# A streaming encoder layer on one core: the low halves of branch B's weights move from VectorE to GpSimd, and the spare pieces are dealt out as two lists

## The chip, the core and the metric

The kernel runs on one core of one Trainium2 chip. Five engines work side by side and meet at semaphores: TensorE (PE, its weight loads PEld), VectorE (DVE), ScalarE (ACT), GpSimd (POOL) and SyncE (SP), which here issues nearly all DMAs in one queue. Each engine takes its instructions in the order in which the program lists them. The metric is the time of one execution on the device in microseconds (us); lower is better. A difference is told as a ratio or in us against the kernel before.

## What is computed

One layer over 2048 new frames ("prompt", 16 tiles of 128 rows) and 8 running streams of 16 frames each ("sample", one tile of 128 rows) with 512 cached positions. A normalised and modulated input is projected; two attention branches run on it; both are gated, projected, merged and added to the input. Branch A is differential softmax attention (4 heads of 2 x 64), branch B stick-breaking attention (8 heads of 64):

```python
def stick_breaking_attention(q, k, v, qpos, kpos):
    z = jnp.einsum('bqhd,bkhd->bhqk', q, k,
                   preferred_element_type=jnp.float32) * (HEAD_DIM_B ** -0.5)
    mask = kpos[None, :] < qpos[:, None]
    log_1m = jnp.where(mask, jax.nn.log_sigmoid(-z), 0.0)
    log_a = jax.nn.log_sigmoid(z) + lax.cumsum(log_1m, axis=3, reverse=True) - log_1m
    a = jnp.where(mask, jnp.exp(log_a), 0.0)
    o = jnp.einsum('bhqk,bkhd->bqhd', a, v, preferred_element_type=jnp.float32)
    return o.astype(v.dtype)
```

The kernel forms the weight as a product of two numbers: sigmoid(z), and the running product of sigmoid(-z) over the later keys. Matrix products want more than 16 bits of precision here, so an f32 operand is written as two f16 numbers, a high half (the value rounded) and a low half (what the rounding lost).

## The kernel before

The work has three stages: normalisation and modulation of the input (to about 140 us), attention (to about 1850 us), and the merge with the samples' attention (to the end).

Attention runs in 8 units, `u` = 0 to 7. An even unit is one head of branch A (`kind` 0), an odd unit is two heads of branch B (`kind` 1). A unit has 17 steps: the samples' projection (`t == NT`, with `NT` = 16), then the 16 tiles `t` = 0 to 15. Step `t` computes scores of 128 queries against the first `t + 1` blocks of 128 keys, so a unit's steps grow. The value products of a step are issued two steps later (`PV_LAG` = 2). The projections (`line`, function `take`) run some five steps ahead of the scores (`LEAD`), so the last steps of a B unit carry projections of the next unit, an A unit, whose rotation (L479, L481, L484) is on POOL and whose splits (L304, L473) are on ACT and DVE.

What a B step does for each of its two heads, from the last chunk of 512 keys to the first: scores on PE into a PSUM bank (L649, L650); two sigmoids on ACT (L123), one into the SBUF buffer `p`, one in place in PSUM; a scan on DVE (L626, function `stick`) that reads the bank, writes the running product to the SBUF buffer `n` and frees the bank. Chunks are gathered in segments of up to 8 blocks, 1024 keys. When a segment has been scanned, `stick_weights` multiplies `p` by `n` on POOL (L632), and `turn` makes the f16 halves in the room of `n`: the high half by a cast on ACT (L582), the low half by a subtraction on DVE (L583). SP then issues one DMA (L590) that transposes both halves into `wt`, from which PE takes its weights for the value products (L710, L711). There are 24 segments for each head of a unit, so 192 in all, 80 of them of 1024 keys and 16 of each shorter length. There are six buffers each for `p` and `n` (`SC_BUFS`), five for `wt` (`WT_BUFS`), three PSUM banks for scores. The samples' tile uses the same functions later, with 8 segments of 640.

The order on each queue is not the program's text alone: the framework lays the instructions out by its own estimate of times, and deals semaphores accordingly. The main loop (from about L1288) decides which pieces a step is given.

Beside this, each step is given pieces of other work. `prepare_unit` (`back`) loads, scales and splits the next unit's weights in the first nine steps of a unit (half of the first parts of these splits are on POOL, L301, the second on DVE, L304). `norms` (`spare`) holds 82 entries in one list: 48 norms (one load of 512 KB and one sum of squares on ACT, L281) of branch weights, output weights and cached values; then 34 stages for cached keys. A stage loads one piece of 512 KB, squares another on ACT, and splits a third: a sum over partitions on PE, four tiny instructions on DVE that make a scale (L867 to L870), the high half on POOL (L301), the low half on DVE (L304), and a store of 512 KB (L875). `spare_at` names the 81 steps that get an entry each, the first of them two: in unit 0 from `t` = 7, in units 2, 4 and 6 all 16 tiles, in units 1, 3 and 5 `t` < 8. In this order the norms take units 0 to 3 and six steps of unit 4; the key stages take the last ten steps of unit 4, eight of unit 5 and all of unit 6.

## Time and profile before

| | |
|---|---|
| median of 3 runs | 2340.57 us (2337.23 to 2343.8) |
| the profiled execution's own time | 2343.11 us |
| its span, first to last instruction | 2341.3 us |
| mean granted TensorE clock | 0.967 of full speed |
| DMA packets moved | 445.30 MB, 190 GB/s on average |

A busy share is the part of a stretch in which an engine executes. A busy PE is not PE at its peak, because matmuls overlap in the records. In a row of groups the columns are the line, the engine, the operation, the buffers written and read, the shape, the count, the busy time, the mean of one in ns, the idle time of the engine just before them and what ended it. In a row of waits they are who waited, for whom, us in total, times, and the longest. In a row of a stretch they are its ends, its length, and the busy time and count of each engine named in its header. A row of a line's instructions gives the shortest, median and longest duration in ns, when the first and the last began, and the shapes.

### The profile page before, as it was taken

To read this page: it belongs to the slowest core of one execution; us is meant where nothing else is said; L and a number is where in the kernel's file an instruction comes from. 1 tells how busy PE (TensorE), PEld (TensorE's weight loads), DVE (VectorE), ACT (ScalarE), POOL (GpSimd) and SP (SyncE) were. 2 spreads that over 40 slices of the span, in tenths; PEclk is the share of its full clock that TensorE was granted. 3 is DMA by queue.
4 is the path that set the end of the run, shared out by engine and by line. 5 is a ranking of instruction groups with operands and counts; after the bars stand their busy time and mean duration, and the time that the engine had idled before them with its cause. 6 is when DMAs were issued, how large, how long until landed. Compare 5 with 4: busy or idle time off the path is not lost. (4 is left out here: it accounts for less than half of the span.)

```text
span 2341.3 us, 41804 instructions
## 1 busy us (share of the span) xinstructions
PE 2102.5 (90%) x14752; PEld 1128.2 (48%) x14752; DVE 1745.7 (75%) x3795; ACT 1624.2 (69%) x3228; POOL 702.6 (30%) x610
## 2 busy tenths in 40 slices
PE   5998899988999898898989988889998689899998
PEld 3654454545555454444544544445454344444443
DVE  4658766779776777977777798887778878677663
ACT  4868677777877777786676786766578666556541
POOL 1223012356400244641033366311335312122111
PEclk8999999999999999999999999999999799999999
DMA  9768667799886778977777789966577899788421
GB/s 335 267 212 222 137 144 174 158 211 198 217 200 146 176 158 202 199 183 183 206 192 185 168 192 229 250 167 165 147 162 168 182 271 260 210 223 215 145 96 55
DMA packets 805827, 445.30 MB, mean 190 GB/s; under 512 B 537354, under 2 KB 744506, under 8 KB 805104
## 3 DMA queue, kind: packets, MB, share of 16 engines
q1 hardware_dynamic: 804668, 442.24, 75.5%
q8 instruction: 115, 1.88, 0.3%
q14 instruction: 96, 0.79, 0.1%
q10 hardware_dynamic: 948, 0.39, 0.1%
HBM read 228.82 MB, written 86.02 MB: 134 GB/s over the span
## 5 line engine op out<-in xcount | busy, mean ns | idle before, releaser
L632 POOL TENSOR_TENSOR sc_p<-sc_p,sc_n 128x127 f32<-128x127 f32 (+7 forms) x192 | 311.3, 1625 | 673.8 <-DVE sc_n L626 650.8
L438 PE MATMUL ps_mm<-wb,hs 128*128 128x512 f16 x1530 | 399.3, 383 | 6.6 <-DMA hs<-hT_d 3.8
L438 PE MATMUL ps_mm<-wa,hs 128*128 128x512 f16 x1590 | 404.3, 380 | 0.8 <-DVE v L304 0.5
L438 PEld LDWEIGHTS <-hs 128*128 128x128 f16 x3120 | 275.6, 99 | 257.0 <-issue 7.8
L626 DVE TENSOR_TENSOR_SCAN sc_n<-ps_s,sc_n,zero_t 128x512 f32<-128x512 f32 x192 | 245.4, 1278 | 72.9 <-ACT ps_s L123 69.2
L649 PE MATMUL ps_s<-k,qst 128*128 128x512 f16 (+3 forms) x640 | 226.7, 355 | 47.2 <-DVE sc_n L626 28.8
L583 DVE TENSOR_TENSOR sc_n<-sc_p,sc_n 128x128 f16<-128x128 f32 (+7 forms) x192 | 213.0, 1115 | 48.2 <-ACT sc_n L582 47.9
L514 PEld LDWEIGHTS <-hs 128*128 128x128 f16 x1632 | 157.1, 99 | 186.9 <-issue 9.6
L514 PE MATMUL ps_t<-wb,hs 128*128 128x512 f16 x1020 | 244.5, 382 | 1.5 <-DVE qst L542 1.5
L123 ACT ACTIVATE sc_p<-ps_s,usc 128x512 f32<-128x512 f32 (+3 forms) x320 | 204.2, 638 | 47.8 <-PE ps_s L650 36.3
L650 PE MATMUL ps_s<-k,qst 128*128 128x512 f16 (+3 forms) x640 | 226.3, 355 | 0.0
L710 PE MATMUL ps_o<-v,wt 128*128 128x128 f16 x1088 | 174.3, 226 | 56.7 <-DMA wt<-sc_n 56.7
L582 ACT CAST sc_n<-sc_p 128x128 f16<-128x128 f32 (+7 forms) x192 | 155.4, 814 | 69.4 <-POOL sc_p L632 69.2
L123 ACT ACTIVATE ps_s<-ps_s,usc 128x512 f32<-128x512 f32 (+3 forms) x328 | 199.2, 607 | 0.0
L1391 PE MATMUL ps_o<-wo,wa 128*128 128x512 f16 x816 | 185.1, 382 | 6.0 <-ACT wo L299 5.3
L710 PEld LDWEIGHTS <-wt 128*128 128x128 f16 x1088 | 106.4, 102 | 122.5 <-DMA wt<-sc_n 68.9
L514 PE MATMUL ps_t<-wa,hs 128*128 128x512 f16 x612 | 157.3, 389 | 6.0 <-ACT qst L542 6.0
L711 PE MATMUL ps_o<-v,wt 128*128 128x64 f16 x1088 | 160.9, 199 | 0.0
L1362 PE MATMUL ps_mm<-wa,wb 128*128 128x512 f16 x510 | 144.2, 390 | 7.8 <-DVE wa L1364 3.4
L568 DVE TENSOR_SCALAR_CACHE_REDUCE sc_p<-ps_s,usc 128x512 f32<-128x512 f32 (+3 forms) x160 | 106.2, 664 | 35.3 <-PE ps_s L650 19.5
L626 DVE TENSOR_TENSOR_SCAN sc_n<-ps_s,zero_t 128x128 f32<-128x128 f32 (+3 forms) x128 | 104.1, 815 | 37.3 <-ACT ps_s L123 36.6
L711 PEld LDWEIGHTS <-wt 128*128 128x128 f16 x1088 | 104.3, 101 | 54.9 <-issue 0.8
(374 smaller groups left out, 4460.3 us busy)
## 6 DMA issues: line engine op xcount, KB each, us to landing
hs<-hT_d SPq DMA_DIRECT2D x130, 512.0 KB, 4.4
g_d<-gt SPq DMA_DIRECT2D x68, 256.0 KB, 4.8
out_dram<-pr SPq DMA_DIRECT2D x204, 64.0 KB, 2.2
wa<-in_w_in_dram SPq DMA_DIRECT2D x40, 256.0 KB, 6.0
o_d<-o SPq DMA_DIRECT2D x136, 64.0 KB, 2.5
wb<-g_d SPq DMA_DIRECT2D x17, 512.0 KB, 3.8
wa<-g_d SPq DMA_DIRECT2D x17, 512.0 KB, 3.4
hs<-o_d SPq DMA_DIRECT2D x17, 512.0 KB, 3.8
```

The lines of the kernel that those rows point to most:

```text
L123: i = S.activation(**kw)
L438: T.matmul(box["p"], box["h"][:, hi, k, :], U["w"][k][:, wi, :], start=(n == 0), stop=(n == 3 * KT - 1))
L514: T.matmul(box["g"][:, 0:gw], box["h"][:, hi, k, :], U["wg"][k // per][:, k % per, wi, :], start=(j == 0), stop=(j == 3 * KT - 1))
L582: S.copy(out=hi, in_=src)
L583: V.tensor_tensor(out=lo, in0=src, in1=hi, op=ALU.subtract)
L626: V.tensor_tensor_scan(out=dst[:, lo : lo + n][:, ::-1], data0=src[:, 0:n][:, ::-1], data1=zero_t[:, 0:1].to_broadcast([P, n]), initial=fi ...
L632: G.tensor_tensor(out=p[:, 0:m], in0=p[:, 0:m], in1=n[:, 1 : m + 1], op=ALU.mult)
L649: T.matmul(p[:, 0:n], qst[:, c, :], kk[:, c, 0:n], start=True, stop=False)
L650: T.matmul(p[:, 0:n], qst[:, 2 + c, :], kk[:, c, 0:n], start=False, stop=not diag)
L710: T.matmul(po[:, c * P : (c + 1) * P], wt[:, wj, :], vt[:, c, :, :], start=first, stop=False)
L711: T.matmul(po[:, c * P : c * P + 64], wt[:, nb + wj, :], vt[:, c, 0, :], start=False, stop=last)
L1391: T.matmul(po, st["y"][:, yi * 8 + k, :], wo[j * 4 + k // 2][:, wi, k % 2, :], start=(n == 0), stop=(n == 3 * KT - 1))
```

## The change

The low half of a B segment is computed on GpSimd in place of VectorE for the 16 prompt tiles; for the samples it stays on VectorE. High half, product, scan, transpose and buffers stay as they are; the scans go on reading PSUM. And `norms` returns two lists in place of one: `spare`, the 48 norms, and `cached`, the 34 key stages. Each has its own set of steps. The norms go to unit 0 from `t` = 7 (nine of them), to `t` = 9 to 15 of units 1 to 5 (seven each), and what is left, four, to the first tiles of unit 6. The key stages go to `t` < 8 of units 1, 3 and 5 (eight each) and to `t` = 9 to 12 of units 2, 4 and 6 (four, four, and the last two). The amount of work is the same.

```diff
@@ turn @@
         if scale is None:
             S.copy(out=hi, in_=src)
-            V.tensor_tensor(out=lo, in0=src, in1=hi, op=ALU.subtract)
+            (G if job["t"] < NT else V).tensor_tensor(out=lo, in0=src, in1=hi, op=ALU.subtract)
         else:
             split(hi, lo, src, scale, S)
@@ norms @@
-        return [lambda x=x: one(*x) for x in srcs] + [lambda k=k: stages(k) for k in range(len(todo) + 2)]
+        return [lambda x=x: one(*x) for x in srcs], [lambda k=k: stages(k) for k in range(len(todo) + 2)]
...
-    spare = norms()
+    spare, cached = norms()
...
-    def spare_at(u, t):
-        return u < 7 and t < NT and (t >= 7 if u == 0 else u % 2 == 0 or t < 8)
+    def norm_at(u, t):
+        return u < 7 and t < NT and (t >= 7 if u == 0 else t >= 9 or u == 6)
+
+    def keys_at(u, t):
+        return u in (1, 3, 5) and t < 8 or u in (2, 4, 6) and 9 <= t < 13
@@ main loop @@
-            if u == 7 and not back and not spare and len(branch_weights) > 1:
+            if u == 7 and not back and not spare and not cached and len(branch_weights) > 1:
                 branch_weight()
...
-            if spare and spare_at(u, t):
-                left = sum(spare_at(*step) for step in steps[n:])
-                for _ in spare[: -(-len(spare) // left)]:
-                    spare.pop(0)()
+            for todo, here in ((spare, norm_at), (cached, keys_at)):
+                if todo and here(u, t):
+                    left = sum(here(*step) for step in steps[n:])
+                    for _ in todo[: -(-len(todo) // left)]:
+                        todo.pop(0)()
...
-        if at[0] == len(line) and not pieces and not spare:
+        if at[0] == len(line) and not pieces and not spare and not cached:
```

## The prediction, as it was put on record before the run

> **What bounds the kernel now.** I read the totals first, then the busy time by stretch, then what TensorE (PE) waited for in the stretches that stood out, and last the two instructions that the edit touches.

> ```profile
> span 2341.3 us, 41804 instructions
> PE 2102.5 (90%) x14752; PEld 1128.2 (48%) x14752; DVE 1745.7 (75%) x3795; ACT 1624.2 (69%) x3228; POOL 702.6 (30%) x610
> ```

> PE is busy nine tenths of the span, so at most 239 us could be won. GpSimd (POOL) has most room. An average hides where the room is, so here are the units 2 to 6 of attention, cut at the first evacuation of each (even units are branch A, odd ones B), the third unit being one B unit from 739 to 971 us:

> ```profile
> core 0: us, PE busy (x) PEld busy (x) DVE busy (x) ACT busy (x) POOL busy (x), PEclk, DMA share, GB/s
> 554.00:739.00 185.00, 178.42 (x1257) 98.24 (x1256) 141.67 (x385) 142.98 (x321) 41.88 (x44) 0.99 0.80 196
> 739.00:971.00 232.00, 211.56 (x1513) 113.14 (x1512) 178.27 (x272) 183.10 (x378) 98.42 (x80) 0.99 0.80 177
> 971.00:1173.00 202.00, 186.72 (x1278) 103.67 (x1276) 157.11 (x429) 142.39 (x314) 51.53 (x54) 0.96 0.79 195
> 1173.00:1416.00 243.00, 219.80 (x1538) 116.63 (x1537) 194.83 (x315) 184.22 (x382) 112.77 (x88) 0.98 0.80 184
> 1416.00:1624.00 208.00, 186.38 (x1286) 103.40 (x1284) 166.71 (x459) 139.71 (x311) 59.87 (x60) 0.98 0.81 209
> ```

> And inside the B units, the middle of unit 1, then the last steps of units 1, 3, 5 and 7:

> ```profile
> 380.00:480.00 100.00, 98.86 (x662) 51.54 (x661) 73.38 (x117) 74.64 (x149) 35.13 (x28) 1.00 0.70 150
> 480.00:580.00 100.00, 84.94 (x669) 46.94 (x668) 89.22 (x140) 77.87 (x157) 60.55 (x48) 0.98 0.97 211
> 900.00:1000.00 100.00, 83.72 (x662) 45.71 (x660) 90.56 (x142) 79.09 (x163) 60.76 (x48) 1.00 0.95 210
> 1340.00:1440.00 100.00, 85.48 (x692) 48.05 (x691) 90.31 (x142) 78.46 (x156) 64.53 (x50) 0.99 0.88 203
> 1780.00:1850.00 70.00, 44.58 (x391) 27.29 (x389) 63.96 (x84) 56.19 (x96) 38.40 (x22) 0.76 0.80 170
> ```

> In the middle PE is the bound (98.9 of 100). In the ends it is not: VectorE (DVE) is at 89 to 91 of 100, at 64.0 of 70 in the last, and PE loses 15.1, 16.3, 14.5 and 25.4 us, 71 us together. What PE waited for there, first from 480 to 580 us, then from 1780 to 1850 us:

> ```profile
> PE ps_s L649 <- DVE sc_n L626: 8.5, 9, 2.6
> PE ps_t L527 <- DVE k L304: 3.0, 3, 1.2
> PE ps_o L710 <- DMA wt<-sc_n: 2.9, 2, 2.0
> ...
> PE ps_o L710 <- DMA wt<-sc_n: 15.1, 11, 3.3
> PE ps_s L649 <- DVE sc_n L626: 5.8, 8, 1.3
> ```

> Scores wait for a PSUM bank that a scan on DVE frees, and the value products for the transpose of weights whose low half DVE made. So in the ends DVE is the bound, and only there.

> **The low halves.** 192 subtractions (L583) leave DVE and go to POOL. What they take on DVE in the first and last of these ends, and beneath that the products (L632) on POOL in the same two:

> ```profile
> 480.00:580.00 100.00, 26.86 (x15) 0.98 0.97 211
> 1780.00:1850.00 70.00, 19.37 (x15) 0.76 0.80 170
> ...
> 480.00:580.00 100.00, 31.02 (x15) 0.98 0.97 211
> 1780.00:1850.00 70.00, 33.23 (x15) 0.76 0.80 170
> ```

> DVE falls from 89.2 to 62.4 in the first and from 64.0 to 44.6 in the last. For the price on POOL I take its product, which like the subtraction has two inputs:

> ```profile
> L632 POOL TENSOR_TENSOR sc_p<-sc_p,sc_n x192: 404/1768/3094, 322.9 to 1841.1; 128x1024 f32<-128x1024 f32 x64, 128x127 f32<-128x127 f32 x16, 128x255 f32<-128x255 f32 x16, 128x383 f32<-128x383 f32 x16
> L632 POOL TENSOR_TENSOR dsc<-dsc x8: 1315/1328/1677, 1943.1 to 2204.4; 128x639 f32<-128x639 f32 x8
> L632 POOL TENSOR_TENSOR sc_p<-sc_p,sc_n 128x1024 f32<-128x1024 f32 x64 | 141.4, 2210 | 216.8 <-DVE sc_n L626 212.2 <-DVE sc_e L232 2.7 <-DVE csc L870 1.9
> L301 POOL TENSOR_SCALAR wa<-wb,csc 128x1024 f16<-128x1024 f32 x11 | 12.9, 1169 | 63.4 <-issue 37.8 <-DVE csc L870 25.6
> L583 DVE TENSOR_TENSOR sc_n<-sc_p,sc_n x192: 260/1084/2994, 326.3 to 1846.8; 128x1024 f16<-128x1024 f32 x80, 128x128 f16<-128x128 f32 x16, 128x256 f16<-128x256 f32 x16, 128x384 f16<-128x384 f32 x16
> L583 DVE TENSOR_TENSOR dsc<-dsc x8: 807/812/820, 1949.7 to 2210.3; 128x640 f16<-128x640 f32 x8
> ```

> Undisturbed, POOL takes 404 ns for 127 columns and 1315 for 639, so 1.78 ns a column, and 2.00 us for 1024. Eighty of that and sixteen each of the seven shorter lengths (0.41, 0.63, 0.86, 1.09, 1.32, 1.54, 1.77, sum 7.6) make 160 + 122 = 282 us. No subtraction from f32 and f16 of this length is in the trace. Bounds: the one-input POOL row above, 1.17 us for 1024, gives 60% of that, 165 us; the disturbed mean of 2.21 gives 312 us. I take 282, since two inputs are what the products have. POOL goes from 703 to about 985 us.

> The product rows spread from 404 to 3094 ns and DVE's from 260 to 2994, and that is a second price:

> ```profile
> L583 DVE TENSOR_TENSOR sc_n<-sc_p,sc_n 128x1024 f16<-128x1024 f32 x9 | 19.2, 2135 | 0.7 <-ACT sc_n L582 0.7
> L626 DVE TENSOR_TENSOR_SCAN sc_n<-ps_s,sc_n,zero_t 128x512 f32<-128x512 f32 x17 | 21.7, 1274 | 0.4
> L473 DVE SCALAR_TENSOR_TENSOR qbuf<-rot,sq,qbuf 128x128 f16<-128x128 f32 x7 | 6.3, 893 | 0.0
> L626 DVE TENSOR_TENSOR_SCAN sc_n<-ps_s,sc_n,zero_t 128x512 f32<-128x512 f32 x192 | 245.4, 1278 | 72.9 <-ACT ps_s L123 69.2
> L473 DVE SCALAR_TENSOR_TENSOR qbuf<-rot,sq,qbuf 128x128 f16<-128x128 f32 x68 | 37.5, 551 | 9.2 <-ACT qbuf L472 9.0
> ```

> The first three are from 500 to 580 us, the others from the whole run. DVE's own rate is (812 - 260) / 512 = 1.08 ns a column, 1.23 us for 1024, but in the end of a unit the subtraction takes 2.14, and the query's split 893 ns against 551. The scan, whose data is in PSUM, takes 1274 against 1278. So DVE and POOL hold each other up where both read two operands from SBUF, and the scans are out of it. After the change the pair product and low half no longer collide; the splits of queries, keys and weights that stay on DVE meet a busier POOL.

> [...]

> Now the end of a unit, 480 to 580 us, engine by engine. DVE 62.4. POOL 60.6, plus 15 low halves, as many as products, mostly of 768 to 1024 columns (1.54 to 2.00), so about 1.85 (27.8), minus what its 15 products lost to collisions (31.0 - 27.8 = 3.2): 85. PE 84.9, ACT 77.9. The floor is 85, a gain of 15. But three engines near 80% that wait for one another in order do not overlap fully, so I take 40% of it, 6 us; ends: 15 gained, or 4 lost if POOL pays the disturbed 2.21 us throughout and its queue adds a wait per step. Three such ends: -18 (-45 to +12). The last, 70 us long: POOL 38.4 + 27.8 - 5.4 = 61 against DVE's 44.6, so POOL is the new bound and 9 us are free; I take -5 (-9 to +4).

> Each low half also lengthens the chain scan, product, cast, low half, transpose, value product. In the short first steps of a B unit nothing covers that; from 321 to 421 us the only wait of PE was

> ```profile
> PE ps_o L710 <- DMA wt<-sc_n: 7.1, 3, 4.4
> ```

> The four shortest lengths cost POOL 0.41, 0.63, 0.86, 1.09 against DVE's 0.26, 0.40, 0.54, 0.67: 1.1 us more, for two heads 2.2 a unit, 9 in four units. A low half that waits for ACT's cast also holds back everything behind it on POOL: the next product, the rotations of branch A's projections, the halving of a key piece. On SP's queue the transpose waits for POOL now, with the next loads behind it. And the halving of a key piece, now among the products of units 1 and 3 too, holds POOL up itself:

> ```profile
> POOL wa L301 <- DVE csc L870: 83.6, 14, 16.8
> L582 ACT CAST sc_n<-sc_p 128x128 f16<-128x128 f32 (+7 forms) x192 | 155.4, 814 | 69.4 <-POOL sc_p L632 69.2
> ```

> Six us on average over 14 times, though unit 5 has this already and loses no more PE time to it than unit 3 (23 and 20 us). I take +7 (0 to +25). In the middle of the units PE at 98.9 covers it.

> **The two lists.** Nothing is added: 48 norms and 34 stages of cached keys stay. Unit 2 had no key stages, unit 4 ten, unit 6 sixteen, and these three A units last 185, 202 and 208 us, so 1.4 to 1.7 us a stage; B unit 5 with eight stages lasts 243 against unit 3's 232 with eight norms. After: eight in each of units 1, 3 and 5, four in 2 and 4, two in 6. By a straight line that is zero. The norms of units 1 to 5 move to the last seven steps; each squares on ACT:

> ```profile
> L281 ACT ACTIVATE junk<-wa 128x1024 f16<-128x1024 f32 x69 | 73.5, 1065 | 31.8 <-DMA wa<-in_x_prompt_dram 11.0 <-DMA wa<-in_cache_b_k_dram 6.5 <-DMA wa<-in_w_in_dram 5.6
> ```

> That is 7.5 us more ACT, with seven loads of 512 KB, where ACT has 22 us free in 100 and DMA is at 0.97; the A units' first steps lose as much. I take -4 for the even spread (-18 to +12).

> **Sum.** -18 - 5 + 7 - 4 = -20 us against the profiled execution's 2343.1 us: 2323. The median of the runs shown, 2340.6, lies 2.5 lower, and I put the prediction there: 2321 us.

> **Rivals.** *POOL takes DVE's place at the same pace.* In 500 to 550 us the steps are bound by DVE now; a last step needs four products and four low halves of 2.0 us, 16 us, before any rotation. If that alone sets the pace, the ends gain nothing and +7 - 4 is left: 2344, no difference. *The ends run at PE's pace:* all 15.1 + 16.3 + 14.5 + 9 = 55 and the lists' -4 come in, the chain costs nothing: 2282. *Slower: POOL's order.* One mechanism: product and low half share one queue, each low half waits there for its cast on ACT (814 ns, above), finished scans wait behind it, the six buffers fill, and scans stop freeing banks. If a third of the 192 casts are not covered by another product, 52 us come on top of the forecast: 2373. It decides from a wait of 20 / 192 = 0.10 us per low half on. For it: POOL at 85 of 100; against it: POOL's order has many products two by two ahead of the low halves, which gives the cast cover.

> **Chances.** Forecast 0.40 (own range 2298 to 2334); PE's pace 0.18; same pace 0.14; POOL's order 0.28. A difference under 0.3% (7 us) can't be told from none. Faster 0.58, same 0.14, slower 0.28. The range runs from just past the full gain to just past the queue's loss, 2279 to 2376.

> **What would show it.** Right: 192 subtractions on POOL at about 2.0 us for 1024 columns; the last 100 us of B units with DVE near 65 and POOL near 85; "L649 <- DVE sc_n" almost gone; A units 4 and 6 shorter, 2 longer. Wrong: POOL over 90 of 100 in the ends with scans waiting for it, longer waits of L710 for wt in the first steps of B units, ACT's casts or squares ending the waits, or key stages that hold POOL's queue.

## The result, and the profile after

| | us |
|---|---|
| kernel before, median of 20 runs | 2339.76 (2332.51 to 2348.25) |
| kernel after, median of 20 runs | 2347.72 (2340.25 to 2355.59) |
| ratio after to before | 1.0033, 95% interval 1.0020 to 1.0045 |
| profiled execution after (its span) | 2340.84 (2339.0) |

The change makes the kernel 8 us slower; the forecast was 2321 us, 20 us faster. The profiled execution of after lies at the short end of its 20 runs. Its trace shows what moved, but not the 8 us; for those the experiments' traces are used further down. The ratios leave out one run in the slow state, of the control before_hs: 3612 us at a mean granted clock of 0.556.

The totals of the page of after:

```profile
span 2339.0 us, 41932 instructions
PE 2106.9 (90%) x14752; PEld 1132.2 (48%) x14752; DVE 1587.5 (68%) x3603; ACT 1622.1 (69%) x3228; POOL 949.3 (41%) x802
```

DVE gave up 158 us and POOL took on 247. The ends of the four B units, in the same stretches as before:

```profile
480.00:580.00 100.00, 92.15 (x710) 50.48 (x709) 75.86 (x124) 78.67 (x158) 80.70 (x63) 1.00 0.86 193
900.00:1000.00 100.00, 94.27 (x715) 51.77 (x714) 68.00 (x108) 80.01 (x159) 79.16 (x61) 0.97 0.87 189
1340.00:1440.00 100.00, 90.48 (x662) 48.83 (x661) 62.79 (x86) 80.31 (x156) 76.44 (x57) 0.97 0.91 203
1780.00:1850.00 70.00, 41.87 (x347) 24.68 (x345) 48.76 (x61) 52.01 (x86) 58.28 (x36) 0.78 0.74 150
```

PE rises from 84.9, 83.7 and 85.5 to 92.2, 94.3 and 90.5: the first three ends went the way that was forecast. The last, where POOL is now at 58 of 70 us, did not: PE is at 41.9, where it had 44.6 before. The same view in steps of 20 us shows what the 100 us hide:

```profile
500.00:520.00 20.00, 18.64 (x149) 10.22 (x147) 15.24 (x18) 17.75 (x34) 18.93 (x15) 1.00 0.88 185
520.00:540.00 20.00, 19.62 (x157) 10.81 (x156) 13.05 (x16) 14.91 (x30) 20.00 (x15) 1.00 0.83 187
540.00:560.00 20.00, 19.07 (x142) 10.29 (x141) 17.07 (x28) 18.52 (x37) 18.36 (x17) 1.00 0.88 191
```

POOL is full for the last 60 us. The forecast's "85 of 100" was near as a mean (80.7) and wrong as a description, because the stretch of 100 us takes in 20 us behind the unit's last product on POOL (L632, at 560.8 us). Units 2 to 6, cut at each first evacuation:

```profile
555.00:745.00 190.00, 173.38 (x1234) 96.63 (x1232) 146.06 (x399) 139.82 (x313) 48.44 (x50) 0.96 0.77 187
745.00:988.00 243.00, 225.64 (x1554) 120.88 (x1553) 152.43 (x267) 186.41 (x385) 167.11 (x132) 0.97 0.86 202
988.00:1186.00 198.00, 179.22 (x1252) 100.58 (x1250) 151.35 (x405) 142.79 (x319) 49.83 (x53) 0.95 0.73 181
1186.00:1436.00 250.00, 226.59 (x1556) 120.06 (x1555) 155.07 (x267) 191.22 (x393) 171.68 (x137) 0.98 0.87 204
1436.00:1619.00 183.00, 172.71 (x1229) 96.31 (x1228) 143.58 (x392) 129.74 (x296) 44.76 (x46) 0.97 0.67 159
```

Unit 6, which lost 14 of its 16 key stages, is 25 us shorter (183 for 208); units 3 and 5 are 11 and 7 longer, unit 4 is 4 shorter and unit 2 is 5 longer. The shift of length from A units to B units is the lists' doing: the kernel with the lists alone, further down, has a unit 6 of 183 us too. The PEclk column is the one to note: units 2, 3 and 4 had 0.99, 0.99 and 0.96 before and have 0.96, 0.97 and 0.95 now.

What POOL's instructions cost, by shape, and what SP's queue waited for:

```profile
L583 POOL TENSOR_TENSOR sc_n<-sc_p,sc_n 128x1024 f16<-128x1024 f32 x80 | 171.9, 2151 | 26.2 <-ACT sc_n L582 25.3
L632 POOL TENSOR_TENSOR sc_p<-sc_p,sc_n 128x1024 f32<-128x1024 f32 x64 | 128.1, 2002 | 83.4 <-DVE sc_n L626 82.4 <-DVE usq L1240 0.7
```
```profile
SPq L590 <- POOL sc_n L583: 91.2, 48, 6.3
SPq L590 <- POOL sc_p L632: 73.6, 41, 4.8
```

The subtraction of 1024 takes 2.15 us (2.00 was taken), the product fell from 2.21 to 2.00. The transposes now wait 165 us for POOL at the head of SP's queue. Before, they waited 66 us for DVE's subtraction, and in the kernel with the lists alone 90 us.

### The profile page after: what moved, and what is told of

It is laid out like the page before. It is cut to its first block, busy times and chain, and to the rows that moved or that the text cites. A ratio compares the mean times of both kernels' runs of the same rounds, so it can differ in the third digit from the quotient of the medians.

```text
span 2339.0 us, 41932 instructions
## 1 busy us (share of the span) xinstructions
PE 2106.9 (90%) x14752; PEld 1132.2 (48%) x14752; DVE 1587.5 (68%) x3603; ACT 1622.1 (69%) x3228; POOL 949.3 (41%) x802
## 5 line engine op out<-in xcount | busy, mean ns | idle before, releaser
L632 POOL TENSOR_TENSOR sc_p<-sc_p,sc_n 128x127 f32<-128x127 f32 (+7 forms) x192 | 291.1, 1519 | 364.0 <-DVE sc_n L626 265.2
L438 PEld LDWEIGHTS <-hs 128*128 128x128 f16 x3120 | 280.8, 99 | 278.5 <-issue 16.9
L438 PE MATMUL ps_mm<-wa,hs 128*128 128x512 f16 x1590 | 397.1, 382 | 7.0 <-DVE v L304 4.0
L438 PE MATMUL ps_mm<-wb,hs 128*128 128x512 f16 x1530 | 392.4, 385 | 2.3 <-DMA hs<-hT_d 2.3
L626 DVE TENSOR_TENSOR_SCAN sc_n<-ps_s,sc_n,zero_t 128x512 f32<-128x512 f32 x192 | 246.0, 1281 | 143.0 <-ACT ps_s L123 134.8
L583 POOL TENSOR_TENSOR sc_n<-sc_p,sc_n 128x128 f16<-128x128 f32 (+7 forms) x192 | 305.4, 1598 | 61.2 <-ACT sc_n L582 58.8
L649 PE MATMUL ps_s<-k,qst 128*128 128x512 f16 (+3 forms) x640 | 226.5, 355 | 47.9 <-DVE sc_n L626 28.4
L123 ACT ACTIVATE sc_p<-ps_s,usc 128x512 f32<-128x512 f32 (+3 forms) x320 | 205.2, 641 | 33.5 <-PE ps_s L650 19.6
L514 PE MATMUL ps_t<-wb,hs 128*128 128x512 f16 x918 | 218.5, 381 | 2.9 <-ACT qst L542 2.9
L123 ACT ACTIVATE ps_s<-ps_s,usc 128x512 f32<-128x512 f32 (+3 forms) x328 | 200.7, 612 | 0.0
L710 PE MATMUL ps_o<-v,wt 128*128 128x128 f16 x1088 | 164.7, 226 | 39.4 <-DMA wt<-sc_n 39.1
L582 ACT CAST sc_n<-sc_p 128x128 f16<-128x128 f32 (+7 forms) x192 | 155.6, 813 | 47.5 <-POOL sc_p L632 47.4
L1395 PE MATMUL ps_o<-wo,wb 128*128 128x512 f16 x816 | 184.0, 379 | 4.2 <-ACT wo L299 1.8
L514 PE MATMUL ps_t<-wa,hs 128*128 128x512 f16 x714 | 171.6, 382 | 7.5 <-ACT qst L542 6.8
L710 PEld LDWEIGHTS <-wt 128*128 128x128 f16 x1088 | 105.3, 102 | 95.8 <-DMA wt<-sc_n 47.3
L711 PE MATMUL ps_o<-v,wt 128*128 128x64 f16 x1088 | 150.8, 198 | 0.0
L1403 POOL TENSOR_TENSOR x<-m,x 128x512 f32<-128x512 f32 x34 | 51.7, 1524 | 234.2 <-DVE m L1399 126.3
L626 DVE TENSOR_TENSOR_SCAN sc_n<-ps_s,zero_t 128x128 f32<-128x128 f32 (+3 forms) x128 | 103.8, 814 | 49.9 <-ACT ps_s L123 39.8
L479 POOL TENSOR_TENSOR rot<-pr,rope 128x256 f32<-128x256 f32 x68 | 54.5, 802 | 191.0 <-DVE qbuf L473 79.2
L1366 PEld LDWEIGHTS <-wb 128*128 128x128 f16 x816 | 79.7, 101 | 105.4 <-issue 24.6
```

The costliest lines, as they stand in the source:

```text
L123: i = S.activation(**kw)
L438: T.matmul(box["p"], box["h"][:, hi, k, :], U["w"][k][:, wi, :], start=(n == 0), stop=(n == 3 * KT - 1))
L514: T.matmul(box["g"][:, 0:gw], box["h"][:, hi, k, :], U["wg"][k // per][:, k % per, wi, :], start=(j == 0), stop=(j == 3 * KT - 1))
L582: S.copy(out=hi, in_=src)
L583: (G if job["t"] < NT else V).tensor_tensor(out=lo, in0=src, in1=hi, op=ALU.subtract)
L626: V.tensor_tensor_scan(out=dst[:, lo : lo + n][:, ::-1], data0=src[:, 0:n][:, ::-1], data1=zero_t[:, 0:1].to_broadcast([P, n]), initial=fi ...
```

## The experiments

Each kernel is compared with the kernel before on the same chip. Where nothing else is said, a diff is against the kernel before.

**The parts, and a change that should do nothing.** Low halves alone, lists alone, low halves on POOL in the last six tiles only, and the 48 norms in reverse order:

```diff
@@ half_only, turn @@
+            (G if job["t"] < NT else V).tensor_tensor(out=lo, in0=src, in1=hi, op=ALU.subtract)
@@ lists_only @@
     the whole change without the line in turn
@@ half_ends, turn @@
+            (G if 10 <= job["t"] < NT else V).tensor_tensor(out=lo, in0=src, in1=hi, op=ALU.subtract)
@@ null_order, norms @@
+        srcs.reverse()
```

> The low halves go to POOL, the one list of spare pieces stays as before. Theory 1 (two parts of opposite sign: the low halves win in the ends of the B units, the two lists lose more in the units that now carry key stages and late norms): 8 to 15 us faster than the kernel before, 2325 to 2332. Theory 2 (POOL's queue: each low half stands behind products and casts and costs what DVE saves): no faster than before, 2340 to 2355. In the profile theory 1 has PE at 92 or more of 100 in the last 100 us of units 1, 3 and 5 and unit 3 no longer than 232 us; theory 2 has unit 3 near the 242 us that it has with the whole change.

> The low halves stay on DVE, the spare pieces are dealt out as two lists. Theory 1: 8 to 20 us slower than before, 2348 to 2360; units 1, 3 and 5 longer, unit 6 about 25 us shorter. Theory 2: 0 to 7 us faster than before, since unit 6 loses 14 stages and units 1 and 3 take theirs where POOL is nearly idle.

> The low halves go to POOL only for the tiles 10 to 15, those in which DVE was at 90 of 100; the one list as before. If the gain comes from the ends alone and the longer chain of the first steps costs some us, this is 0 to 7 us faster than the low halves on POOL for all tiles; if POOL's load in the ends eats the gain, it is the same as the kernel before within 5 us.

> The kernel before with its 48 norms taken in the reversed order, same count, sizes and steps. No theory has a reason for a difference: within 4 us of the kernel before. If it differs by 7 us or more, then a mere new layout of the instructions moves the time by that much, and differences of that size between kernels here say nothing about a mechanism.

Measured: low halves alone 1.0065 (1.0040 to 1.0090), lists alone 0.9969 (0.9953 to 0.9986), last tiles only 1.0050 (1.0031 to 1.0070), reversed norms 0.9935 (0.9913 to 0.9957). The product of the first two is 1.0034, the whole change 1.0033: these two parts add. The loss is the low halves' (2362 us, slower than either theory asked), and most of it is there with the last six tiles alone. The reversed norms, an edit that was to do nothing, win 0.65%: order alone moves this kernel as far as any part of the change, so a single small difference proves little here. What follows leans on differences that come back in several kernels.

**Where the loss sits.** The stretches of units 1 to 7 in the kernel with the low halves alone, cut as above:

```profile
320.50:552.60 232.10, 220.17 (x1536) 116.96 (x1535) 135.49 (x229) 183.10 (x379) 156.45 (x126) 0.99 0.82 179
552.60:751.70 199.10, 177.34 (x1232) 96.84 (x1230) 141.95 (x379) 142.82 (x320) 44.17 (x47) 0.96 0.73 180
751.70:984.20 232.50, 221.74 (x1542) 117.46 (x1540) 139.14 (x230) 184.65 (x380) 156.12 (x126) 0.99 0.80 180
984.20:1191.10 206.90, 184.20 (x1266) 102.72 (x1265) 155.46 (x421) 142.36 (x319) 52.24 (x56) 0.93 0.72 184
1191.10:1434.20 243.10, 226.26 (x1564) 119.97 (x1563) 159.60 (x277) 184.94 (x381) 174.88 (x138) 0.98 0.82 190
1434.20:1637.70 203.50, 182.99 (x1225) 100.50 (x1224) 164.29 (x451) 138.41 (x311) 61.50 (x59) 0.94 0.80 206
1637.70:1877.90 240.20, 203.99 (x1487) 111.47 (x1485) 157.64 (x256) 170.32 (x334) 164.55 (x118) 0.91 0.71 154
```

and the two that the prediction did not show of before, units 1 and 7:

```profile
320.60:553.90 233.30, 213.55 (x1518) 113.91 (x1516) 178.44 (x274) 183.73 (x379) 98.49 (x80) 0.99 0.79 176
1623.70:1854.00 230.30, 196.38 (x1419) 107.66 (x1417) 185.34 (x294) 168.35 (x332) 95.46 (x69) 0.92 0.70 154
```

Length minus PE busy is PE's idle time. In B units 1, 3 and 5 it falls from 19.8 + 20.4 + 23.2 = 63 us to 11.9 + 10.8 + 16.8 = 40: this is the gain that was forecast. Yet these units are no shorter (707.7 us, 708.3 before): what PE gained it spent on work of the unit behind, 73 matmuls more in them. The A units 2, 4 and 6 have 98 matmuls fewer than before and should be shorter; they last 609.5 us for 595. Their idle time goes from 6.6 + 15.3 + 21.6 = 43 us to 21.8 + 22.7 + 20.5 = 65. And their clock falls from 0.99, 0.96 and 0.98 to 0.96, 0.93 and 0.94. Unit 7 is 10 us longer. These are single executions: this one of half_only is 21.5 us longer than that of before, the medians differ by 16.7.

One such gap, in the view of stretches of the same kernel, with the longest wait of PE from 560 to 700 us:

```profile
595.38:598.80 3.42, 0.10 (x2) 0.00 (x0) 2.63 (x11) 3.42 (x9) 2.19 (x4) 1.00 0.66 186
598.80:602.21 3.41, 2.26 (x6) 0.89 (x7) 1.21 (x4) 3.41 (x9) 0.02 (x1) 0.51 0.80 211
602.21:605.62 3.41, 3.41 (x10) 1.21 (x8) 1.32 (x4) 1.29 (x4) 0.00 (x0) 0.50 1.36 256
```
```profile
PE ps_mm L438 <- DMA hs<-hT_d: 4.5, 1, 4.5
```

PE stands 4.5 us, 3.3 of them in the first of these rows, because a projection's input arrives late; SP issued that load at 596 us. Its queue had stood from 565 to 572 us for a split of weights on DVE (L304) and had been busy with loads, transposes and stores since. In the 6.8 us that follow the granted clock is 0.50 to 0.51: PE works, at half speed (in the trace of the kernel before, 128x512 matmuls of L438 that follow one another begin 426 ns apart at half clock, the median of 25, and 216 ns apart at full clock, the median of 3191). No such wait for `hs` was in this stretch before. Units 4 and 6 have the same gap, 3.9 us at 1032 and 4.0 us at 1473; in all PE waits 17.0 us for `hs`, where it waited 4.0 before.

**Is it the rotations, the first tiles, or order?**

```diff
@@ half_rot = half_only and, in the projections @@
-                G.tensor_tensor(out=rot..., in0=x4,
+                R = V if U["u"] and (t == NT or t < 6) else G
+                R.tensor_tensor(out=rot..., in0=x4,
     (L481 and L484 the same)
@@ half_early, turn @@
+            (G if job["t"] < 10 else V).tensor_tensor(out=lo, in0=src, in1=hi, op=ALU.subtract)
@@ half_null = half_only, lists_null = lists_only, both with, in norms @@
+        srcs.reverse()
```

> Low halves on POOL for all tiles, one list; besides, the three rotations of the projections of the sample tile and of tiles 0 to 5 of units 2, 4 and 6 go from POOL to DVE: these are the projections that run in the ends of the B units, and with them POOL sheds 7 x 2.2 = 15 us per hand-over. Theory 1 (the cost of the low halves sits at the hand-over from a B unit to an A unit: rotations wait behind products and low halves on POOL, PE runs dry there and its clock is lowered): 15 to 25 us faster than low halves alone, 2338 to 2348, unit 2 back from 199 to 187 us or less, clock 0.965 or more. Theory 2 (a chance of the layout, with nothing to do with POOL's queue): 2355 to 2368.

> Low halves on POOL for tiles 0 to 9 only, on DVE for 10 to 15; one list. Theory 1: the hand-over is as before, so within 5 us of the kernel before, and the costs of the two halves of the tiles add up (the tiles 10 to 15 alone cost 13 us, all of them 17). Theory 3 (the cost is the longer chain of each segment, wherever it is): about half of the 17 us, 2352 to 2356.

> Low halves on POOL for all tiles, one list with its norms in the reversed order. If the reversal is worth its 0.65% by itself, this is 15 us faster than low halves alone, 2345 to 2350. If the reversal's gain was a chance of the layout, this lies anywhere within 10 us of 2360.

> Low halves on DVE, two lists, norms in the reversed order. If the two gains (0.31% and 0.65%) are separate, 2322 to 2326 and faster than both kernels of the case; if they are the same gain or chances of the layout, 2332 to 2340.

Measured: half_rot 1.0048 (1.0031 to 1.0066), half_early 0.9993 (0.9980 to 1.0007), half_null 1.0011 (0.9997 to 1.0024), lists_null 0.9930 (0.9907 to 0.9953). On POOL in the first ten tiles, where a unit's steps are short, the low halves cost nothing. On top of the reversed norms they cost 1.0011 / 0.9935 = 0.76%, so their price does not hang on that order. The lists' gain does: on top of the reversed norms they add nothing (0.9930 to 0.9935; 2328.0 us, between the two forecasts). Moving the first rotations to DVE did not help. Why can be read in the last 60 us before the last product (L632) of unit 1, half_only first, then half_rot:

```profile
500.20:560.20 60.00, 56.40 (x449) 31.34 (x446) 44.22 (x58) 47.41 (x91) 56.20 (x45) 1.00 0.92 201
```
```profile
504.00:564.00 60.00, 45.06 (x389) 25.34 (x387) 58.09 (x62) 44.01 (x83) 43.13 (x24) 1.00 0.78 168
```

With the rotations on DVE, it is DVE that is full again, 58.1 of 60, and PE falls from 56.4 to 45.1 us.

**Late loads, or POOL's load?** Projection inputs fetched two steps ahead, with and without the low halves; and the low halves of tiles 14 and 15 left on DVE:

```diff
@@ half_hs = half_only, before_hs = before, both with @@
-H_AT = 2
+H_AT = 4
-            if i == H_AT and not at_hand and m + 1 < len(steps) and steps[m + 1] not in ahead:
-                fetch_h(*steps[m + 1])
+            if i == H_AT and not at_hand:
+                for k in (m + 1, m + 2):
+                    if k < len(steps) and steps[k] not in ahead:
+                        fetch_h(*steps[k])
@@ half_13, turn @@
+            (G if job["t"] < 14 else V).tensor_tensor(out=lo, in0=src, in1=hi, op=ALU.subtract)
```

> Low halves on POOL for all tiles, one list; the projections' inputs are loaded two steps ahead instead of one. Theory 4 (the loads stand in SP's queue behind transposes that now wait for POOL, so PE waits for them: 17 us instead of 4 with low halves alone): those waits fall under 5 us and 8 to 15 us come back, 2346 to 2352. Theory 5 (the evacuations of branch A find their buffers still held by the last B segments, or PE loses its clock for other reasons): within 4 us of low halves alone, 2355 to 2364.

> The kernel before with the projections' inputs loaded two steps ahead, as a control. PE waited 4 us for these loads, so 0 to 4 us faster by both theories; more than that would say that the earlier load helps by itself and proves nothing on the low halves.

> Low halves on POOL for tiles 0 to 13 and on DVE for the last two of a unit, one list. Theory 6 (the cost is POOL's backlog at the hand-over from a B unit to an A unit, whoever waits for it): the backlog is gone and a part of the gain in the ends stays, 2330 to 2343, unit 2 at 188 us or less. If instead POOL's load in tiles 10 to 13 costs as much as that in 14 and 15, half of the 15 us stays: 2350 to 2354.

Measured: half_hs 1.0038 (1.0024 to 1.0053), before_hs 0.9962 (0.9948 to 0.9975), half_13 0.9971 (0.9956 to 0.9986). Earlier loads help both kernels alike, and the low halves cost 1.0038 / 0.9962 = 0.76% on top of them: late loads are a wait of their own, not the low halves' price. Taking only two tiles of 16 back to DVE turns the loss into a small gain.

**A place, or a load?** Only tiles 14 and 15 on POOL; another piece of work taken from POOL; and the whole change with the edit of half_13, alone and with the other two gains:

```diff
@@ half_last, turn @@
+            (G if 14 <= job["t"] < NT else V).tensor_tensor(out=lo, in0=src, in1=hi, op=ALU.subtract)
@@ half_cut = half_only and, in the next unit's weights @@
-                split(..., S if i % 2 else G)
+                split(..., S if i % 2 or u else G)
@@ after_13, against after @@
-            (G if job["t"] < NT else V).tensor_tensor(out=lo, in0=src, in1=hi, op=ALU.subtract)
+            (G if job["t"] < 14 else V).tensor_tensor(out=lo, in0=src, in1=hi, op=ALU.subtract)
@@ best_mix = after_13 with srcs.reverse() and the loads of half_hs @@
```

> Low halves on POOL for the tiles 14 and 15 of a B unit alone, on DVE for 0 to 13; one list. Theory 6 (all of the cost is made by the last two tiles, at the hand-over): slower by as much as all tiles on POOL or more, 0.6 to 1.0%, 2357 to 2368, and the last low half of unit 1 ends 15 us or more after its last scan (6 us before the change). If the cost needs POOL's load from the tiles 10 to 13 ahead of it, under 0.4%.

> Low halves on POOL for all tiles, one list; the high halves of the next unit's weights, which stand in POOL's queue ahead of the last low half in units 2, 4 and 6, are made on ACT instead. Theory 7 (POOL's queue holds the last low half back by what stands ahead of it, 4.4 us of splits and their wait): the last low half of units 1 and 3 ends 8 to 13 us after the last scan instead of 18, and 4 to 10 us come back, 2352 to 2358. Theory 8 (what hurts is that POOL needs 2 x 2.0 us for each last segment, whatever else stands there): under 3 us come back.

> The whole change, but with the low halves of the tiles 14 and 15 on DVE as before. If theory 6 holds and the parts add up (0.9969 for the lists, 0.9971 for the low halves up to tile 13): 0.994, 2328 to 2334, faster than the kernel before and than the change. If they do not add up, 2336 to 2345.

> The whole change with the low halves of the tiles 14 and 15 on DVE, the norms in the reversed order and the projections' inputs loaded two steps ahead. If the four gains add up (0.994, 0.9935 and 0.9962): 0.984, 2303 to 2312. If they overlap, 2315 to 2330.

Measured: half_last 0.9980 (0.9964 to 0.9996), half_cut 1.0085 (1.0063 to 1.0107), after_13 0.9932 (0.9914 to 0.9949), 2325.67 us, where 0.994 was expected, and better than both kernels of this case; best_mix 1.0050 (1.0032 to 1.0067) where 2303 to 2330 us was expected. Tiles 14 and 15 alone cost nothing, tiles 0 to 13 alone cost nothing, together they cost 0.65%: not a place, a load. With two lists the same two tiles are worth as much (1.0033 to 0.9932). The last 60 us of unit 1 of half_13, then of half_last:

```profile
497.90:557.90 60.00, 52.58 (x427) 29.09 (x424) 53.55 (x69) 50.17 (x96) 48.67 (x36) 0.97 0.98 204
```
```profile
497.10:557.10 60.00, 53.90 (x425) 29.73 (x425) 52.03 (x67) 50.81 (x93) 47.27 (x36) 0.97 0.92 201
```

PE, DVE, ACT and POOL are all below 90% there. half_cut leaves POOL at 94%, as in half_only. It did not test theory 7. The splits that it took away stood ahead of the last low half on POOL (563.8 to 568.2 us in half_only); now they stand on ACT, ahead of that low half's cast. Rows of half_cut in order of time, first POOL, then ACT (start, length, what; in brackets the idle time before it and what ended it):

```profile
568.87 2.13 POOL L583 TENSOR_TENSOR sc_n<-sc_p,sc_n 128x1024 f16<-128x1024 f32 x1 [5.92 <-ACT sc_n L582]
```
```profile
561.70 2.56 ACT L299 ACTIVATE wb<-wa,sw 128x512 f16<-128x512 f32 x4 [0.64 <-DVE sw L235]
564.17 1.93 ACT L299 ACTIVATE wa<-wa,sw 128x512 f16<-128x512 f32 x3
567.76 1.03 ACT L582 CAST sc_n<-sc_p 128x1024 f16<-128x1024 f32 x1
```

So that low half ends 19.9 us after the last scan, where theory 7 asked for 8 to 13 and half_only has 17.6.

**One head of two.** Tiles 10 to 15 with one head's low halves on POOL and one on DVE, with one list and with the whole change; and after_13 with the reversed norms:

```diff
@@ half_c0, turn, against before; after_c0, turn, against after @@
+            (G if job["t"] < 10 or job["t"] < NT and job["c"] == 0 else V).tensor_tensor(out=lo, in0=src, in1=hi, op=ALU.subtract)
@@ after_13_null, against after_13, norms @@
+        srcs.reverse()
```

> Low halves on POOL for tiles 0 to 9 and, of tiles 10 to 15, for the first head alone; the second head's stay on DVE; one list. Theory 9 (the loss comes when POOL is full in the ends: 96 to 98% of the last 60 us with all low halves there, 81 to 86% where a part stays on DVE): POOL at 80 to 87%, and 0.1 to 0.4% faster than the kernel before, 2333 to 2341. Theory 10 (any low half on POOL in the last tiles makes the loss, or a chance of the layout): 0.3 to 0.6% slower, 2348 to 2356.

> The whole change, with the second head's low halves of the tiles 10 to 15 on DVE. Theory 9 and the lists' gain of 0.3% added: 0.5 to 0.8% faster than the kernel before, 2323 to 2331. Theory 10: 2340 to 2348.

> The whole change with the low halves of the tiles 14 and 15 on DVE and the norms in the reversed order, loads as before. If it is the earlier loads that spoilt the mixture of all, 0.985 to 0.991, 2309 to 2322; if the reversed order does not go together with the rest, 2340 or more.

Measured: half_c0 0.9986 (0.9972 to 1.0000), after_c0 1.0032 (1.0017 to 1.0047), after_13_null 0.9931 (0.9908 to 0.9954). The first is at the small end of what the load theory asked for, and hardly clear of no difference. The second breaks it: POOL is not full and the kernel is slower (2323 to 2331 us was expected, 2355.97 measured). The third shows that the reversed norms add nothing to after_13, so what spoilt best_mix is the earlier loads. That they do so because of the two lists is not shown: best_mix differs from the kernels that they helped in its low halves and its order too.

**All kernels in one account.** From each trace, worked out over attention (139 us to the last value product): the time in which no matmul of PE is recorded, and half the time in which the granted clock was a half ("to clock"). Beside them, the mean share of POOL and DVE in the last 60 us before the last product (L632) of units 1, 3 and 5. The ratio is of medians, the rest of the one profiled execution; that of half_cut is 11 us under its median and that of half_early 8 us over.

| kernel | ratio | POOL, DVE % | PE idle | to clock |
|---|---|---|---|---|
| before | 1 | 71, 97 | 162 | 51 |
| half_only | 1.0065 | 94, 74 | 161 | 72 |
| half_ends | 1.0050 | 94, 76 | 161 | 68 |
| half_null | 1.0011 | 95, 75 | 149 | 65 |
| half_hs | 1.0038 | 95, 75 | 148 | 72 |
| half_cut | 1.0085 | 94, 76 | 160 | 60 |
| after | 1.0033 | 93, 75 | 152 | 58 |
| half_rot | 1.0048 | 72, 97 | 173 | 46 |
| best_mix | 1.0050 | 82, 88 | 159 | 60 |
| after_c0 | 1.0032 | 82, 92 | 156 | 58 |
| half_early | 0.9993 | 72, 96 | 155 | 56 |
| half_c0 | 0.9986 | 82, 88 | 147 | 55 |
| half_last | 0.9980 | 81, 87 | 144 | 56 |
| half_13 | 0.9971 | 81, 89 | 154 | 43 |
| lists_only | 0.9969 | 70, 96 | 159 | 46 |
| before_hs | 0.9962 | 71, 97 | 148 | 52 |
| null_order | 0.9935 | 71, 98 | 147 | 52 |
| after_13 | 0.9932 | 82, 91 | 142 | 51 |
| after_13_null | 0.9931 | 85, 90 | 151 | 41 |
| lists_null | 0.9930 | 69, 96 | 149 | 39 |

What remains of attention after both columns is 1499 to 1509 us in 19 of the 20, 1517 in half_rot: the two columns hold most of what differs. Against its own control the low half with POOL full costs no idle time but clock: half_only to before, -1 us idle and +21 to clock; half_hs to before_hs, 0 and +20; half_null to null_order, +2 and +13. Where in attention this happens shows when the same account is made by units (cut at the first evacuation on DVE), in us against the control:

| kernel, control | PE idle, units 1, 3, 5 | PE idle, units 2, 4, 6 | to clock, units 2, 4, 6 |
|---|---|---|---|
| half_only, before | -24 | +22 | +19 |
| half_ends, before | -23 | +20 | +19 |
| half_null, null_order | -33 | +34 | +20 |
| half_hs, before_hs | -26 | +34 | +16 |
| after, lists_only | -22 | +17 | +17 |
| after_c0, lists_only | -13 | +10 | +7 |
| after_13, lists_only | -20 | +8 | +9 |
| after_13_null, lists_null | -15 | +14 | +5 |
| half_c0, before | -17 | -1 | -2 |
| half_last, before | -16 | +1 | +2 |
| half_13, before | -8 | -10 | -7 |

In the first five pairs POOL is full: most or all of what the ends of the B units win comes back as idle time in the A units, and the clock is lost on top. With two lists, the kernels that share show the same at about half the size; with one list they don't. The gaps are longer too: all six kernels with POOL full have 76 to 83 us of attention in gaps over 2 us, before has 57, the others 51 to 70.

The clock alone does not order the kernels. Over all runs the mean granted clock is 0.958 to 0.962 in the six with POOL full and 0.965 to 0.966 in before; but half_c0 and half_last have 0.961 and 0.962 and are faster, with little idle time (147 and 144 us). half_rot is slower with DVE full, the most idle time and a clock of 0.967. best_mix loses 19 us more to the clock than after_13_null. And the table ends with attention: behind it best_mix and after_c0 take 495.5 and 496.5 us where before takes 487.1, which is most of what their profiled executions lose against it (8 of 10 us, 9 of 14). No run took that last stage apart.

## Why the prediction was wrong, step by step

**"I take 40% of it, 6 us" for each of three ends, -18, and -5 for the last: this is the step that failed.** Its first half held: DVE fell, PE rose from 84.9 to 92.2 of 100, and the wait of scores for a scan all but went, from 8.5 us to the first of these rows of after, 480 to 580 us (the second was 2.9):

```profile
PE ps_s L649 <- DVE sc_n L626: 0.9, 1, 0.9
PE ps_o L710 <- DMA wt<-sc_n: 0.9, 1, 0.9
```

But the sum took PE's lost time in the ends as a gain in the kernel's time. In half_only 24 us of idle in the B units came back as 22 us of idle in the A units behind them, and unit 7 became 10 us longer where 5 were to be won. The unit behind has no price in the sum: the +7 names rotations that are held back on POOL, but counts only the longer chain of the first steps.

**The price that was missing is the clock.** Before, PE's gaps in the first three ends were short and dealt by DVE's pace: 18 or 19 in each 100 us, the longest 2.6, 2.9 and 2.3 us, PE at 85% and a clock of 0.98 to 1.00, so they cost their own length. With POOL full they gather behind the unit's end, and a long gap costs its length and the half clock after it: 21 us in half_only, 19 of them in units 2, 4 and 6. That is an account of the recorded clock, which comes back in five pairs above; no run changed the clock alone. The route from POOL to the gaps is open. Some of the gaps are late loads (17.0 us in half_only); with earlier loads PE waits 8.6 us for them, but the A units are as idle (65 us in half_only and in half_hs), and the price is 0.76%. Nor does SP's wait for POOL decide: it is 165 us in after and 162 in half_13, which gains.

**POOL at "85" of 100.** The mean was near and the stretch too long: 57 of the last 60 us. The rival "POOL takes DVE's place at the same pace" came nearest with 2344 us, where 2347.72 was measured, but by luck: it has the ends gain nothing, and PE's idle time there fell by 22 us or more against the controls. The slower rival, that low halves wait for their cast, has its wait in after (58.8 us, 0.31 us for each of 192, above its 0.10). But half_13 has 44.6 us of it and half_only 42.3, and one gains where the other loses, so that wait did not decide.

**282 us for the low halves** were 305: 2.15 us in place of 2.00 for 1024, an error of 8% in the right place. That DVE and POOL hold each other up where both read two SBUF operands came out as said: POOL's product went from 2210 to 2002 ns once the subtraction had left DVE. In the trace of before, DVE's subtraction of 1024 takes 1221 ns where POOL is busy for under 5% of it (mean of 30) and 1814 where POOL is busy for over half of it (37); the scan of 512, which reads PSUM, takes 1279 (111) and 1275 (55), the split of `v` (L304), with one operand in PSUM, 341 (44) and 342 (85). On POOL's side one input is enough: beside L301 the split of `wb` on DVE (L304) takes 1141 ns (7), without POOL 739 (9).

**+7 for the early chain** was too much: half_early 0.9993, no difference.

**-4 for the lists** had the right sign with the norms in their old order: lists_only 0.9969, -7 us, and -4 is inside its interval. With the reversed norms the lists are worth nothing. Unit 6 became 25 us shorter, more than the 14 stages at 1.4 to 1.7 us each that left it.

## What to carry to other kernels

Before moving work to an idle engine, look at its load in the last steps where the work would land, not in a mean that takes in the next stage; fill no engine there, but share (tiles 0 to 13 here, 0.9971, in place of all 16, 1.0065; with two lists and the reversed norms sharing neither won nor lost, 0.9931 to 0.9930). Price gaps of TensorE by how they lie: many short ones cost their length here (up to 2.9 us in the first three ends of before, at a clock of 0.98 to 1.00), the same time gathered in a few costs the half clock behind each as well (half_only: idle time of 161 us for 162, and 21 us more to clock). And measure an edit that should do nothing beside the change: here the order of equal loads was worth 0.65%, so a part's sign is only known against its own control.

## What the runs showed of the hardware that was not expected

Open are four things. How a full POOL makes the gaps in the unit behind. Why reversing 48 loads of equal size takes 15 us of PE's idle time away; no run took that apart. Why the earlier loads lose in best_mix (0.9931 to 1.0050) and gain in the two kernels with one list. And why one head of two on POOL is right with one list and not with two.
